# Hybrid decoder layer on one core: the first prompt tile's choice ahead of the sample rows' mixers, its gathers of peer_u beside them, its gathers of peer_v in the second tail

## The chip, the core and the metric

The kernel runs on one core of a Trainium2 chip. The metric is the device time of one execution in microseconds (us). The engines are TensorE (PE; PEld is its loading of weights), VectorE (DVE), ScalarE (ACT), GpSimd (POOL) and SyncE (SP, which issues most DMAs). Gathers of table rows ("indirect DMAs") are issued by POOL.

## What is computed

One decoder layer over 512 prompt rows and 32 sample rows (8 requests of 4), of width 1024. Cut to what matters here:

```
z = x @ w_in -> latent attention (8 heads) and mLSTM memory (4 heads)
  sample rows: latent attention over 2048 cached rows of each request (by page_table),
               and one step of the stored memory state_C
x = layer_norm(ALPHA * x + concat(heads) @ w_out)
x = layer_norm(ALPHA * x + mem_attend(x, ...))          # w_mq, 256 memory tokens, w_mo
q = x @ w_pq; s1, s2 = q @ sub_k1, q @ sub_k2           # 8 heads, 128 keys each
e, g = top 16 of the sums of top 16 of s1 and top 16 of s2; g = softmax
a = g * gelu(x . peer_u[e])                             # 8 x 16 rows of a table of 16384
x = layer_norm(ALPHA * x + sum(a * peer_v[e]))
```

## The kernel before, in words

The prompt is four tiles of 128 rows (0 to 3); the sample rows are tile 4. Group 0 is tile 0 with the sample rows, group 1 is tiles 1, 2 and 3. The last step ("peer") is done in two ways. For tiles 1 and 2 both tables are multiplied whole ("dense"): 128 blocks of peer_u (`u_block`, products `ph`) and 128 blocks of peer_v (`v_block`, products `yd`). For tiles 0, 3 and 4 the chosen rows are gathered: 128 gathers of peer_u and 128 of peer_v for tiles 0 and 3, 32 and 32 for tile 4, each of 128 rows of 1024 floats. A gathered buffer of peer_u (`ru`) is multiplied with the rows and summed by one DVE instruction, a "dot". A gathered buffer of peer_v (`rv`) is summed by eight matmuls `y<-rv,Z`, a "y group", for which DVE writes the weights into `Z`.

The program is one list per engine, in the order in which the code is written, with a paced side list beside it: `te` counts the estimated time of the TensorE instructions that the code writes, and when more than `te.every` has gathered, one step of a second list is written there (`te.start(steps, every)`; `te.finish()` writes the rest at once). `v` does the same by DVE's instructions. Which step stands where on each engine is thus fixed when the program is made.

The stages of before, in order:

- `mixers(0)`: projections, latent attention and mLSTM of group 0. Beside it the keys and values of the memory tokens (`memory`, products `pw`), one step for every 7.0 us.
- `sample_matrix` (the stored state `Ch`, 4 updates of it) and `sample_latent`: 16 iterations, each with four gathers `kvb` of cached rows, 16 transposes of them, copies `kts`, products with `qb` and `qrb`, a maximum (`sst`), the exponential `se`, its transposes, a copy `sPT` and the products `kvb,sPT`.
- `tail("0")` for tile 0: w_out, a layer norm, the memory attention, a layer norm, w_pq (`wz`) and the scores (`sub_k`). The scheduler mixes its first part and the memory's rest into the iterations of `sample_latent`.
- `choices[0].rest()` and `.done()`: the top 16 of tile 0, on DVE, ending with the indices `eT` for the gathers.
- `mixers(1)`, and beside it, after `SKIP` steps, the choice's end and `hidden()`: 128 gathers of `ru` for tile 0 and their dots, one for every 2.6 us.
- `tail("1")` for tiles 1, 2, 3 and the sample rows, with what is left of `hidden()` and, from the end of the tail on, `G`: the other 160 gathers of `ru` and all 288 of `rv`, tile 0's `rv` first.
- The choices of tiles 4, 1, 2 and 3, with the first 40 u blocks; the gates of tiles 1 and 2; and the loop over the 128 v blocks with the other 88 u blocks and the rest of `G`.

Of the kernel before, what the change touches and what calls it, by code (L numbers as in the profile page):

```python
# [18 lines left out]
PSUM = bass.MemoryType.PSUM  # L19
# [174 lines left out]
def program(ctx, tc, I, O, dbg=None):  # L194
# [58 lines left out]
    PN = []  # L253
# [2 lines left out]
    PS = stage.enter_context(tc.tile_pool(name="psum", bufs=4, space=PSUM))  # L256
    stackN, stackC, stackM, stackG, stackX = (ExitStack() for _ in range(5))
    PN.append(stackN.enter_context(tc.tile_pool(name="psum sample", bufs=1, space=PSUM, side="right")))
    SL = stackN.enter_context(tc.tile_pool(name="slat", bufs=1, side="right"))
    DR = ctx.enter_context(tc.tile_pool(name="scratch", bufs=1, space=bass.MemoryType.DRAM))  # L260

    def ps(n=512, name="pm"):
# [5 lines left out]
    def ps3(n=512, name="pc"):  # L268
        return PN[-1].tile([128, n], F32, name=name, tag="pc", bufs=1)
# [42 lines left out]
    right = {}  # L312
# [1164 lines left out]

    def found(i, nh, ef, gt):
        np_ = TOPK * nh
        p = ps3()  # L1480
        te.behind(te.transpose(p[:np_, :128], ef[:, 0], ident))
        te.transpose(p[:np_, 128:256], gt.rearrange("p h k -> p (h k)"), ident)
        if i in DT:
            te.transpose(p[:, 256:384], ef[:, 1], ident)
            v.tensor_copy(iT[i][:, 0:2], p.rearrange("p (a b) -> p a b", b=256)[:, :, :128])
            v.tensor_copy(gT[i], p[:, 128:256])
            s.activation(iT[i][:, 2], p[:, 256:384], AF.Copy, scale=-1.0)
            s.activation(iT[i][:, 3], p[:, 128:256], AF.Copy, scale=-1.0)
        else:
            n = 128 * nh // PH  # L1490
            for a in range(PH // nh):
                v.tensor_copy(eT[i][np_ * a:np_ * a + np_], p[:np_, n * a:n * a + n])
                s.copy(gT[i][np_ * a:np_ * a + np_], p[:np_, 128 + n * a:128 + n * a + n])
# [137 lines left out]
            for w in vs:  # L1631
                self.v_group(*w[1:])

    def hidden(stk):


        X = stk.enter_context(tc.tile_pool(name="hidden", bufs=1, side="right"))
        us = []

        def dot():  # L1640
# [177 lines left out]
    def chooser(T):  # L1818
        def f():
            if T is T0:  # L1820
                stackN.close()
                right["DX"] = ctx.enter_context(tc.tile_pool(name="dense rows", bufs=1, side="right"))
                right["weights"] = ctx.enter_context(tc.tile_pool(name="weights", bufs=1, side="right"))
                right["XG"] = stackX.enter_context(tc.tile_pool(name="rows1", bufs=1, side="right"))
                right["xT1"] = transposed(1, right["XG"])
            else:
                te.finish()
                stackH.close()
                G.open(stackG)
            X = stackC.enter_context(tc.tile_pool(name="choose", bufs=1, side="right"))  # L1830
            for i, c, P in T:
                choices[i] = Choice(i, P, X)
            return X
        return f
# [5 lines left out]
    first_rows(xt0)  # L1840
    for a in range(2):
        nc.scalar.dma_start(lnb0[a], ln_src(0, a))
    MS = stackM.enter_context(tc.tile_pool(name="mixstate", bufs=1))
    Kh = MS.tile([128, H, SEQ], F32, name="Kh")
    vh = MS.tile([128, 4, 512], F32, name="vh")
    mkT = MS.tile([128, MH, SEQ], F32, name="mkT")
# [1 line left out]
    va = MS.tile([128, 4, MH, 129], F32, name="va")  # L1848
    v.memset(va[:, :, :, 128:129], 1.0)

    EVERY0 = 7.0
    with tc.tile_pool(name="group0", bufs=1) as Gp:
        with weights("weights0", 4):
            xT0 = transposed(0, Gp, xt0)
            rows = sample_index(SL)
            te.start(memory(MM, lnb0, xt0), EVERY0)
            with tc.tile_pool(name="q0", bufs=1) as Gq:
                mixT0 = mixers(0, xT0, Gp, Gq)
            with tc.tile_pool(name="smat", bufs=1) as X:
                sample_matrix(X)  # L1860
        sample_latent(SL, *rows)
        te.finish()
        stackF.close()
        with weights("weights0t", 10), tc.tile_pool(name="tail0", bufs=1) as X:
            tail("0", T0, mixT0, Gp, X, chooser(T0))
    DX, XG = right["DX"], right["XG"]
    for i in DT:
        iT[i] = DX.tile([128, 4, 128], F32, name=f"iT{i}")
    LATER = 200
    EVERY = 2.6  # L1870
    EVERY2 = 2.6
    EVERY3 = 1.25
    EVERY4 = 1.75
    EVERY5 = 1.65
    SKIP = 4
    NZ = 2
    W1 = weights("weights1", 2)
    xT1 = right["xT1"]
    with tc.high_priority(-LATER):
        choices[0].rest()  # L1880
    stackC.close()
    G = Gather(stackG, [[(4, 0)], [(3, 32 * q) for q in range(4)]], 3, 6, 3)
    stackH = ExitStack()
    UB0 = 8
    PN.append(stackN.enter_context(tc.tile_pool(name="psum choose", bufs=1, space=PSUM, side="right")))

    def chosen():
        for _ in range(SKIP):
            yield
        choices[0].done()  # L1890
        yield
        yield from hidden(stackH)

    te.start(chosen(), EVERY)
    with tc.tile_pool(name="q1", bufs=1) as Gq:
        mixT1 = mixers(1, xT1, XG, Gq)
    for t, m in zip(mixS, mixT1):
        s.copy(m[:, :, TG:], t)
    W1.close()
    stackM.close()  # L1900
    te.every = EVERY2
    with weights("weights2", 6), tc.tile_pool(name="tail1", bufs=1) as X:
        xT2 = tail("1", T1, mixT1, XG, X, chooser(T1))
    stage.close()
# [14 lines left out]

    v.start(ahead(), EU1)  # L1920
    G.strict = True
    te.start(G.steps(), EVERY3)
    for i in (4,) + DT + (3,):
        choices[i].rest()
        choices[i].done()
# [50 lines left out]
```

## Time and profile before

| | |
|---|---|
| median of 3 runs | 2143.56 us (2138.07 to 2146.85) |
| the profiled execution's own time | 2154.7 us |
| its span (first to last instruction) | 2152.9 us |
| PE busy | 1878.7 us (87%) |
| DVE busy | 1421.5 us (66%) |
| POOL busy | 836.5 us (39%) |
| moved by DMA | 624.85 MB, 290 GB/s over the span |
| mean granted clock of PE | 0.933 |

The span is what the rows below divide; 1.8 us of the execution's own time lie around it. The profiled execution is 0.5% longer than the median. [...]

### The profile page before, as it was taken

The page shows a single profiled execution, that of the slowest core. Times are in us where ns is not written, and L with a number is a line of the kernel's source. Part 1 is how long each engine was busy: PE and PEld are TensorE (multiplying, and loading weights), DVE is VectorE, ACT ScalarE, POOL GpSimd, SP SyncE. Part 2 cuts the span into 40 slices and gives each one's busy share as a digit, 9 for nine tenths or more (in the row PEclk, how much of TensorE's full clock was granted, in tenths as well). Part 3 has the DMA queues.
Part 4 walks back from the last instruction along what each step waited for, and adds up shares of the span by engine and source line. Part 5 has one row for each costly group of instructions (what it writes and reads, how often), then busy time and mean ns, then how long its engine had stood idle before and what let it go on. Part 6 is the DMA issues. An engine that isn't in the chain of part 4 may idle for free. (4 is left out here: it accounts for less than half of the span.)

```text
span 2152.9 us, 32053 instructions
## 1 busy us (share of the span) xinstructions
PE 1878.7 (87%) x11579; PEld 1437.4 (67%) x11579; DVE 1421.5 (66%) x3650; ACT 676.2 (31%) x1349; POOL 836.5 (39%) x715
## 2 busy tenths in 40 slices
PE   6998989878888778688999998879979979999997
PEld 4875656766865666366765675658858767777764
DVE  5234324497778786437899687767666757777666
ACT  2121222232234221212312565434423433444332
POOL 3010233015644424215035444346545646665641
PEclk9988999999978879988999999989989999999999
DMA  9635675728965859756489999999999999999996
GB/s 320 217 88 138 187 242 184 243 82 269 320 227 177 305 161 355 242 207 218 114 280 350 355 383 390 385 338 399 405 329 371 405 342 369 405 405 405 398 370 228
DMA packets 212960, 624.85 MB, mean 290 GB/s; under 512 B 23314, under 2 KB 87890, under 8 KB 198082
## 3 DMA queue, kind: packets, MB, share of 16 engines
q0 software_dynamic: 94272, 327.45, 42.3%
q1 hardware_dynamic: 107120, 279.95, 37.1%
q10 hardware_dynamic: 11410, 15.41, 2.1%
q8 instruction: 92, 1.51, 0.3%
q14 instruction: 66, 0.54, 0.1%
HBM read 592.58 MB, written 30.14 MB: 289 GB/s over the span
## 5 line engine op out<-in xcount | busy, mean ns | idle before, releaser
L241 DVE SCALAR_TENSOR_TENSOR ru<-ru,xr 128x1024 f32<-128x1024 f32 x288 | 349.2, 1220 | 178.7 <-DMA ru<-in_peer_u,idx 138.4
L1516 POOL DMA_INDIRECT rv<-in_peer_v,eT x288 | 340.5, 1182 | 297.4 <-PE y L245 231.9
L1516 POOL DMA_INDIRECT ru<-in_peer_u,idx x160 | 219.8, 1374 | 356.3 <-DVE ru L241 193.2
L1663 POOL DMA_INDIRECT ru<-in_peer_u,idx x128 | 161.5, 1262 | 179.2 <-DVE ru L241 112.2
L245 PE MATMUL ph<-xT2h,utl 128*128 128x256 f32 x704 | 202.8, 288 | 16.9 <-DVE utl L241 16.9
L245 PE MATMUL ph<-xT2l,uth 128*128 128x256 f32 x704 | 202.6, 288 | 0.0
L245 PE MATMUL y<-rv,Z 128*32 128x512 f32 x1152 | 171.8, 633 | 34.4 <-DVE Z L241 19.7
L245 PE MATMUL ph<-xT2h,uth 128*128 128x256 f32 x704 | 200.9, 285 | 0.0
L245 PE MATMUL yd<-vtl,ah 128*128 128x512 f32 x512 | 167.5, 404 | 32.4 <-DVE vtl L241 31.7
L328 ACT CAST vth<-vt 128x1024 fp32r<-128x1024 f32 x128 | 134.4, 1050 | 117.7 <-DMA vt<-in_peer_v 59.1
L245 PE MATMUL yd<-vth,ah 128*128 128x512 f32 x512 | 164.4, 399 | 2.3 <-DVE xa L241 1.4
L241 DVE TENSOR_TENSOR vtl<-vt,vth 128x1024 fp32r<-128x1024 f32 x128 | 156.4, 1222 | 14.5 <-ACT vth L328 12.7
L245 PE MATMUL yd<-vth,al 128*128 128x512 f32 x512 | 164.0, 398 | 0.0
L245 PE MATMUL ph<-xw,ut 128*128 128x256 f32 x640 | 154.5, 387 | 1.2 <-ACT h L1763 1.2
L245 PEld LDWEIGHTS ph<-xT2h,utl 128*128 128x128 f32 x704 | 134.8, 191 | 28.0 <-DVE utl L241 18.7
L328 ACT CAST uth<-ut 128x1024 fp32r<-128x1024 f32 x88 | 92.5, 1051 | 187.3 <-PE ph L245 125.9
L245 PEld LDWEIGHTS ph<-xw,ut 128*128 128x128 f32 x640 | 116.4, 191 | 47.5 <-issue 29.3
L245 PEld LDWEIGHTS yd<-vtl,ah 128*128 128x128 f32 x512 | 95.3, 190 | 77.3 <-DVE vtl L241 40.5
L245 PEld LDWEIGHTS ph<-xT2h,uth 128*128 128x128 f32 x704 | 136.0, 193 | 15.3 <-issue 11.7
L245 PEld LDWEIGHTS ph<-xT2l,uth 128*128 128x128 f32 x704 | 135.6, 193 | 11.7 <-issue 8.4
L245 PEld LDWEIGHTS yd<-vth,al 128*128 128x128 f32 x512 | 96.4, 190 | 35.0 <-issue 15.1
L1086 POOL DMA_INDIRECT kvb<-in_pool_lat,ixk x64 | 63.2, 987 | 135.4 <-PE pn L245 120.2
(542 smaller groups left out, 3712.5 us busy)
## 6 DMA issues: line engine op xcount, KB each, us to landing
vt<-in_peer_v SPq DMA_DIRECT2D x62, 1024.0 KB
ut<-in_peer_ut SPq DMA_DIRECT2D x44, 1024.0 KB
ut<-in_peer_ut SPq DMA_DIRECT2D x40, 512.0 KB
Gd<-stg SPq DMA_DIRECT2D x8, 1984.0 KB
Gt<-Gd SPq DMA_DIRECT2D x31, 512.0 KB
wz<-in_w_z SPq DMA_DIRECT2D x30, 512.0 KB
wo<-in_w_out SPq DMA_DIRECT2D x16, 512.0 KB
wz<-in_w_mq SPq DMA_DIRECT2D x16, 512.0 KB
```

Source lines behind the costliest of these rows:

```text
L241: return lambda out, *a, **k: self.count(f(out, *a, **k), 0.06 + math.prod(out.shape[1:]) / 960)
L245: return self.count(self.e.matmul(out, l, r, **kw), math.prod(r.shape[1:]) * (0.42e-3 if r.dtype == F32R else 1.7e-3))
L328: s.copy(hi, src)
L1086: g.indirect_dma_start(out=t.rearrange("p a b -> p (a b)"), out_offset=None, in_=I["pool_lat"], in_offset=bass.IndirectOffsetOnAxis(ap=ixk ...
L1516: self.last = g.indirect_dma_start(out=t, out_offset=None, in_=I[table], in_offset=bass.IndirectOffsetOnAxis(ap=idx, axis=0))
L1663: g.indirect_dma_start(out=t, out_offset=None, in_=I["peer_u"], in_offset=bass.IndirectOffsetOnAxis(ap=idx[:, k:k + 1], axis=0))
```

## The change

`sample_matrix` and `sample_latent` are written after `tail("0")` and after tile 0's choice. The memory's steps run every 3.2 us and are finished right after `mixers(0)`. `hidden()` starts before `sample_latent`, goes on through `mixers(1)` and is finished at its end. `G` (the gathers for tiles 4 and 3 and tile 0's `rv`) starts ahead of `tail("1")`. Pools are moved to make room; the paces change.

```
-    EVERY0 = 7.0
+    EVERY0 = 3.2
...
                 mixT0 = mixers(0, xT0, Gp, Gq)
-            with tc.tile_pool(name="smat", bufs=1) as X:
-                sample_matrix(X)
-        sample_latent(SL, *rows)
         te.finish()
         stackF.close()
         with weights("weights0t", 10), tc.tile_pool(name="tail0", bufs=1) as X:
             tail("0", T0, mixT0, Gp, X, chooser(T0))
...
-    EVERY = 2.6
-    EVERY2 = 2.6
+    EVERY = 2.4
+    EVERY2 = 2.3
     EVERY3 = 1.25
-    EVERY4 = 1.75
+    EVERY4 = 2.55
     EVERY5 = 1.65
-    SKIP = 4
+    SKIP = 10
...
     with tc.high_priority(-LATER):
         choices[0].rest()
     stackC.close()
...
+    with tc.tile_pool(name="smat", bufs=1) as X:
+        sample_matrix(X)
     te.start(chosen(), EVERY)
+    with tc.tile_pool(name="slat", bufs=1) as X:
+        sample_latent(X, *rows)
...
+    xT1 = transposed(1, XG)
+    W1 = weights("weights1", 2)
     with tc.tile_pool(name="q1", bufs=1) as Gq:
         mixT1 = mixers(1, xT1, XG, Gq)
...
     W1.close()
+    te.finish()
     stackM.close()
-    te.every = EVERY2
+    stackH.close()
+    G.open(stackG)
+    te.start(G.steps(), EVERY2)
     with weights("weights2", 6), tc.tile_pool(name="tail1", bufs=1) as X:
         xT2 = tail("1", T1, mixT1, XG, X, chooser(T1))
...
     G.strict = True
-    te.start(G.steps(), EVERY3)
+    te.every = EVERY3
```

Three places show what moves. On PE, one iteration of `sample_latent` before: the rows with `wo,mixT` are tile 0's w_out, and those with `x` its transposes.

```order
282 L245 MATMUL pn<-kvb,sPT 32x256 x8
283 L248 MATMUL pn<-cst_75,kvb 128x128 x16
284 L245 MATMUL pn<-kts,qb 32x256 x3
285 L245 MATMUL pm<-wo,mixT 128x256
286 L245 MATMUL pn<-kts,qb 32x256 x5
287 L245 MATMUL pn<-krT,qrb 32x128 x8
288 L248 MATMUL pn<-cst_75,se 128x128 x2
289 L248 MATMUL pm<-cst_75,x_3008 128x128 x4
290 L245 MATMUL pn<-kvb,sPT 32x256 x8
```

The same engine in the changed kernel, two iterations:

```order
225 L245 MATMUL pn<-kvb,sPT 32x256 x8
226 L248 MATMUL pn<-cst_81,kvb 128x128 x16
227 L245 MATMUL pn<-kts,qb 32x256 x8
228 L245 MATMUL pn<-krT,qrb 32x128 x8
229 L248 MATMUL pn<-cst_81,se 128x128 x2
230 L245 MATMUL pn<-kvb,sPT 32x256 x8
231 L248 MATMUL pn<-cst_81,kvb 128x128 x16
232 L245 MATMUL pn<-kts,qb 32x256 x8
```

Nothing of the memory, of tile 0's tail or of `mixers(1)` stands between the iterations now; all of `memory` stands inside `mixers(0)`, and tile 0's whole tail before the first iteration.

On DVE, one iteration of the changed kernel (`ru,hh` is a dot of tile 0, the other rows are the iteration's own):

```order
578 L241 SCALAR_TENSOR_TENSOR ru,hh<-ru,xr 128x1024
579 L241 COPY kts<-pn 128x512
580 L241 SCALAR_TENSOR_TENSOR ru,hh<-ru,xr 128x1024
581 L241 COPY kts<-pn 128x512
582 L241 TENSOR_REDUCE sst<-pn 128x1
583 L241 TENSOR_TENSOR sst<-sst 128x1
584 L241 TENSOR_TENSOR sst<-sst,scr 128x1
585 L241 SCALAR_TENSOR_TENSOR ru,hh<-ru,xr 128x1024
586 L241 SCALAR_TENSOR_TENSOR sst<-sst 128x1
587 L241 SCALAR_TENSOR_TENSOR ru,hh<-ru,xr 128x1024
588 L241 SCALAR_TENSOR_TENSOR ob<-ob,sst,pn 128x256
```

Before, no dot stood in `sample_latent`. Now 56 of tile 0's 128 do, three or four to an iteration, and POOL's list has three to five `ru` gathers behind each four `kvb` gathers of 13 iterations. The other 72 stand in `mixers(1)`.

On DVE in the stage of the choices, in the changed kernel (`tv`, `ti`, `rep` and `cd` are steps of a top 16; the dots are tile 4's):

```order
1505 L241 TENSOR_TENSOR cd<-tv_8336 128x8x16
1506 L241 MATCH_REPLACE rep<-tv_8336,sc_8338 128x128
1507 L241 SCALAR_TENSOR_TENSOR ru,hh<-ru,xr 128x1024
1508 L241 MAX tv_8336<-rep 128x8
1509 L241 TENSOR_TENSOR cd<-tv_8336 128x8x16
1510 L241 MAX_INDEX ti_8337<-tv_8336,rep 128x8
1511 L241 SCALAR_TENSOR_TENSOR ru,hh<-ru,xr 128x1024
1512 L241 MATCH_REPLACE rep<-tv_8336,sc_8338 128x128
```

Before, no dot stood among the choices. By the order of the lists, the counts of each stage go as follows (before, then after):

| | `tail("1")` | choices | gates | v loop |
|---|---|---|---|---|
| dots | 73, 0 | 0, 32 | 19, 37 | 141, 91 |
| y groups | 13, 54 | 25, 26 | 24, 8 | 82, 56 |

## Rows read from the trace of the kernel before

**Rows 1.** Windows by stage: start:end, length, busy time of each engine, clock, DMA.

```profile
core 0: us, PE busy (x) PEld busy (x) DVE busy (x) ACT busy (x) POOL busy (x), PEclk, DMA share, GB/s
0.00:166.00 166.00, 142.27 (x849) 117.73 (x853) 65.12 (x254) 32.48 (x101) 27.28 (x35) 0.90 0.61 203
166.00:373.00 207.00, 177.78 (x1587) 126.62 (x1586) 76.01 (x210) 41.97 (x105) 55.24 (x58) 0.95 0.65 192
373.00:441.00 68.00, 60.01 (x411) 53.61 (x403) 38.23 (x154) 16.79 (x49) 0.57 (x1) 0.95 0.61 207
441.00:720.00 279.00, 232.29 (x1201) 190.19 (x1202) 223.53 (x606) 89.08 (x191) 123.06 (x104) 0.87 0.69 223
720.00:1035.00 315.00, 246.34 (x1575) 186.97 (x1574) 194.72 (x415) 70.72 (x126) 98.44 (x85) 0.87 0.72 245
1035.00:1200.00 165.00, 154.79 (x779) 106.08 (x777) 148.46 (x791) 36.51 (x78) 57.45 (x56) 0.99 0.76 269
1200.00:1346.00 146.00, 135.85 (x879) 98.17 (x877) 113.53 (x310) 89.87 (x262) 62.32 (x64) 1.00 0.97 375
1346.00:2153.00 807.00, 729.36 (x4320) 558.03 (x4320) 561.85 (x917) 298.78 (x437) 412.11 (x315) 0.96 0.99 370
```

**Rows 2.** Windows, PE alone: tiles pw (memory); pn (`sample_latent`), two stretches; pm.

```profile
166.00:373.00 207.00, 42.74 (x288) 0.95 0.65 192
...
0.00:166.00 166.00, 17.64 (x131) 0.90 0.61 203
166.00:373.00 207.00, 97.68 (x1060) 0.95 0.65 192
...
166.00:373.00 207.00, 37.48 (x175) 0.95 0.65 192
```

**Rows 3.** Timeline of one latent iteration: start, length, engine, what ended its wait.

```profile
303.81 2.10 PE L248 MATMUL pn<-cst,kvb 128*128 128x128 f32 x16
...
309.94 0.43 DVE L241 TENSOR_REDUCE sst<-pn 128x1 f32<-128x256 f32 x1 [3.87 <-PE pn L245]
...
313.00 1.07 PE L245 MATMUL pn<-kvb,sPT 128*32 128x256 f32 x16
314.00 0.77 PE L248 MATMUL pn<-cst,kvb 128*128 128x128 f32 x5
```

**Rows 4.** The page's costliest groups: dots and two kinds of gathers.

```profile
L241 DVE SCALAR_TENSOR_TENSOR ru<-ru,xr 128x1024 f32<-128x1024 f32 x288 | 349.2, 1220 | 178.7 <-DMA ru<-in_peer_u,idx 138.4
...
L1663 POOL DMA_INDIRECT ru<-in_peer_u,idx x128 | 161.5, 1262 | 179.2 <-DVE ru L241 112.2
...
L1086 POOL DMA_INDIRECT kvb<-in_pool_lat,ixk x64 | 63.2, 987 | 135.4 <-PE pn L245 120.2
```

**Rows 5.** Windows: from the last `sub_k` to tile 0's first gather.

```profile
441.00:490.50 49.50, 40.82 (x210) 34.18 (x211) 44.06 (x185) 17.32 (x33) 6.26 (x11) 0.90 0.29 94
```

**Rows 6.** The tile `Ch`, its updates on DVE: lengths, first and last start.

```profile
L241 DVE TENSOR_TENSOR Ch<-Ch,pm x12: 158/681/689, 202.6 to 221.2; 128x512 f32<-128x512 f32 x8, 128x8 f32<-128x8 f32 x4
```

**Rows 7.** Waits in the v loop (1346 to 2153): us in total, times, longest.

```profile
PE yd L245 <- DVE vtl L241: 31.7, 16, 13.7
PE ph L245 <- DVE utl L241: 16.9, 9, 4.8
...
DVE ru L241 <- DMA ru<-in_peer_u,idx: 124.0, 57, 9.6
```

**Rows 8.** Windows, PE alone: 10 us of `tail("1")` at each of two clocks.

```profile
850.00:860.00 10.00, 6.50 (x24) 0.53 1.02 408
870.00:880.00 10.00, 6.41 (x40) 1.00 0.53 178
```

**Rows 9.** Windows, the best 100 us of the v loop.

```profile
1800.00:1900.00 100.00, 98.70 (x640) 78.62 (x638) 70.20 (x111) 41.77 (x60) 62.01 (x44) 1.00 1.03 407
```

**Rows 10.** Windows of the tile Z: PE (y groups), PEld, DVE (weights written), POOL.

```profile
720.00:1035.00 315.00, 15.53 (x88) 2.82 (x88) 2.19 (x13) 0.34 (x2) 0.87 0.72 245
...
1346.00:2153.00 807.00, 96.40 (x672) 13.69 (x672) 13.34 (x82) 0.00 (x0) 0.96 0.99 370
```

More of the change, by code (lines that the diff above doesn't have):

```diff
@@ L258, in program @@
     PN.append(stackN.enter_context(tc.tile_pool(name="psum sample", bufs=1, space=PSUM, side="right")))
-    SL = stackN.enter_context(tc.tile_pool(name="slat", bufs=1, side="right"))
+    stackH, stackS = ExitStack(), ExitStack()
+    XH = stackH.enter_context(tc.tile_pool(name="hidden", bufs=1))
+    MS = stackM.enter_context(tc.tile_pool(name="mixstate", bufs=1))
+    SL = stackS.enter_context(tc.tile_pool(name="sample", bufs=1))
     DR = ctx.enter_context(tc.tile_pool(name="scratch", bufs=1, space=bass.MemoryType.DRAM))
@@ L1479, in found @@
         np_ = TOPK * nh
-        p = ps3()
+        p = ps3() if i else ps2()
         te.behind(te.transpose(p[:np_, :128], ef[:, 0], ident))
@@ L1632, in steps, with hidden @@
                 self.v_group(*w[1:])
-    def hidden(stk):
-        X = stk.enter_context(tc.tile_pool(name="hidden", bufs=1, side="right"))
+    def hidden(X):
         us = []
@@ L1820, in f @@
             if T is T0:
-                stackN.close()
                 right["DX"] = ctx.enter_context(tc.tile_pool(name="dense rows", bufs=1, side="right"))
[L1823 to L1829, printed above, removed]
             X = stackC.enter_context(tc.tile_pool(name="choose", bufs=1, side="right"))
@@ L1842, in program @@
         nc.scalar.dma_start(lnb0[a], ln_src(0, a))
-    MS = stackM.enter_context(tc.tile_pool(name="mixstate", bufs=1))
     Kh = MS.tile([128, H, SEQ], F32, name="Kh")
@@ L1865, in program @@
             tail("0", T0, mixT0, Gp, X, chooser(T0))
-    DX, XG = right["DX"], right["XG"]
+    DX = right["DX"]
     for i in DT:
@@ L1869, in program @@
     LATER = 200
-    EVERY = 2.6
-    EVERY2 = 2.6
+    EVERY = 2.4
+    EVERY2 = 2.3
     EVERY3 = 1.25
-    EVERY4 = 1.75
+    EVERY4 = 2.55
     EVERY5 = 1.65
-    SKIP = 4
+    SKIP = 10
     NZ = 2
-    W1 = weights("weights1", 2)
-    xT1 = right["xT1"]
+    UB0 = 8
     with tc.high_priority(-LATER):
@@ L1881, in program @@
     stackC.close()
[L1882 to L1885, printed above, removed]
     def chosen():
@@ L1891, in chosen @@
         yield
-        yield from hidden(stackH)
+        yield from hidden(XH)
+    with tc.tile_pool(name="smat", bufs=1) as X:
+        sample_matrix(X)
     te.start(chosen(), EVERY)
+    with tc.tile_pool(name="slat", bufs=1) as X:
+        sample_latent(X, *rows)
+    stackS.close()
+    stackN.close()
+    G = Gather(stackG, [[(4, 0)], [(3, 32 * q) for q in range(4)]], 3, 6, 3)
+    PN.append(stackN.enter_context(tc.tile_pool(name="psum choose", bufs=1, space=PSUM, side="right")))
+    right["weights"] = ctx.enter_context(tc.tile_pool(name="weights", bufs=1, side="right"))
+    XG = right["XG"] = stackX.enter_context(tc.tile_pool(name="rows1", bufs=1, side="right"))
+    xT1 = transposed(1, XG)
+    W1 = weights("weights1", 2)
     with tc.tile_pool(name="q1", bufs=1) as Gq:
```

## The prediction, made before the changed kernel was run

> **What bounds the kernel now.** I read the windows by stage first, then what PE waits for in the longest stage, then one iteration of `sample_latent` in time. The windows [rows 1] show that no single engine bounds the kernel: PE is busy for 142 + 178 + 60 of the first 441 us, and its share stays between 0.78 and 0.95 until the end. What changes is what keeps it from 1. Up to 441 us PE runs short of input only for 61 us in all. In the stage of the choices (1035 to 1200) DVE is busy for 148.5 of 165 us, as full as PE. In the v loop (1346 to 2153) the DMA share is 0.99 and PE idles for 807 - 729 = 78 us. The rows of waits there [rows 7] name DVE's halves of the weights (`vtl` 31.7 us, `utl` 16.9 us), but DVE itself waits 124 us for gathered rows of peer_u: its list is in order, so a dot whose gather is late holds back the halves behind it. The best 100 us of that loop [rows 9] have PE busy for 98.7 at full clock. So the v loop is bound by PE with a surcharge that the gathers impose, and it is what the change lightens.
>
> The iterations of `sample_latent` are a chain of short dependent steps: in one that starts at 303.81, the next starts at 314.00, 10.2 us later [rows 3]. PE's own work for it is 97.68 / 16 = 6.1 us by the tile pn [rows 2]. The rest of PE's 178 us in that stretch is memory (42.74 us) and tile 0's tail with odds and ends (37.48 us) [rows 2]. That other work is the cover of the chain, and the change takes it away.
>
> **The change part by part.**
>
> *To the start of `mixers(1)`, now 441 us.* (a) `mixers(0)`: memory's 42.74 us come in, the prelude of `sample_latent` (17.64 us [rows 2]) goes out, and about 5 us of memory fall into PE's 24 idle us of that stage: 166 + 43 - 18 - 5 = 186. (b) Tile 0's tail: the 68 us of 373 to 441 [rows 1] and what stood in the iterations, at most 37.48 us by pm. Part of that belongs to other pieces, but its layer norm now stands uncovered, so I take the whole: 105 us, which also holds the iterations' last products and the transposes for group 1 that now come behind. (c) Choice, then `sample_matrix`, both on DVE with nearly nothing of PE beside them. Between the last `sub_k` and the first gather 49.5 us passed with DVE busy for 44 [rows 5], `mixers(1)` among it; I take 30 for the choice. The updates of `Ch` ran from 202.6 to about 222, 20 us [rows 6]. Sum 50, bounds 40 and 64. (d) The prelude: 17.64 us of PE and its waits, 22. (e) Sixteen iterations alone. Without cover the chain is a little shorter than 10.2 us, since about a microsecond of w_out stood between the last product and the maximum: 9.5. Onto DVE come 56 dots, 3.5 for each iteration, at 1.22 us [rows 4] and about 0.08 for reading the sum: 4.6 us. DVE has long gaps in an iteration, but a dot in front of `kts`, of the maximum or of `sPT` delays the chain by what is left of it. I take 1.5 us for all of them: 11.0 for each, 176. The bounds are 9.5 (all dots hidden) and 14.1 (none hidden). POOL is below that: four kvb at 0.99 and 3.5 ru at 1.26 us [rows 4] make 8.4. Sum: 186 + 105 + 50 + 22 + 176 = 539, which is **+98**; the bounds of (c) and (e) alone make +64 to +162.
>
> *`mixers(1)`* loses the choice (30 us of DVE) and 11 dots (83 in the trace's window, 72 by the lists). PE is busy for 232 of 279 us and DVE for 224 [rows 1], so DVE's relief buys only waits: **-12**, bounds -30 and 0.
>
> *`tail("1")`* gets 43 more y groups (54 by the lists, against 88 matmuls, 11 groups, in the trace) and loses its dots. A group costs 15.53 / 11 = 1.41 us here, 96.40 / 84 = 1.15 in the v loop [rows 10]: 49 to 61 us of PE. PE idles for 69 of this stage's 315 us [rows 1], mostly for weights; a group written ahead of a matmul whose weights are late lies in that wait. I let a little over half of them hide: **+25**, bounds 0 and +60, the upper one if the gathers make the weights later by as much as the groups hide.
>
> *Choices and gates.* 32 dots come into a stage where DVE is busy for 148.5 of 165 us: 32 x 1.30 = 42, and layer norms of the finished tiles, less the 16 us that DVE has free: +35. The gates lose 16 y groups at about 1.2 us and gain 18 dots, with DVE busy for 113 of 146 us and DMA at 0.97 with about as many gathers as before (69 against 64): 0. Together **+35**, bounds +20 and +50.
>
> *The v loop* loses 26 y groups x 1.15 = 30 us of PE, and 50 dots x 1.30 = 65 us of DVE. Of the 102 gathers fewer, each 128 x 1024 x 4 bytes, come 53.5 MB; at the window's 370 GB/s they are 145 us of DMA, so DMA stops being full, and the gathers that remain land earlier. I take two thirds of PE's 78 idle us as won (52), and 3 us from the clock, 0.96 here [rows 1]: **-85**. Bounds: -50 (the groups and a quarter of the idle time) and -137 (groups, all idle time, and 0.04 x 729 = 29 us of clock).
>
> Sum: 98 - 12 + 25 + 35 - 85 = +61. The profiled execution took 2154.7 us, so the changed one takes 2216; the median of before stands at 2143.56 / 2154.7 = 0.995 of its profiled execution, which gives **2205 us** as a median. Put shortly: 128 dots and 102 gathers are moved to where DMA and DVE are free, but the chain that they are moved beside is laid bare, and its cost appears whole.
>
> **The rivals.**
>
> *The v loop gives back all that it can, and the iterations hide the dots: faster.* The best 100 us [rows 9] speak for it: with gathers in time, PE is never idle and at full clock. The v loop is then at -137 and the iterations at 9.5 us (-24 on my sum), `tail("1")` hides all but 10 us of its groups. 61 - 52 - 24 - 15 = -30: **2113 us**. It decides from the point at which the v loop gains 146 us with all else as I have it, or 130 with the iterations at 10 us. Against it: 91 dots stay in the loop, each still ahead of a half that PE needs.
>
> [...]
>
> *The cover is replaced: no change.* If the choice, 30 us, and `sample_matrix`, 20, run in part beside tile 0's own last products and the prelude (their lists are in order on each engine, but the engines are not bound to each other), (c) and (d) shrink by 30, and with the v loop at -115 the sum is +1: **2145 us**.
>
> **How the numbers follow.** I give my forecast (2150 to 2245) a chance of 0.62, the low clock 0.10, no change 0.10, and faster 0.18. A measurement of this kernel can tell about 0.5% (11 us) from no change. The forecast and the low clock are both slower: 0.72. The likeliest time is 2205. The range takes in the bounds of the iterations upward without the whole of the low clock, and most of the faster rival downward: 2122 to 2262.
>
> **What would show it.** In the profile after, `wt1`, the first weights of `mixers(1)`, should start at about 539 us (505 to 600). From the first `kvb` transpose to the last `kvb,sPT` there should be about 176 us, with PE busy for near 55% and dots between `kts` and the maximum. A stretch of about 50 us ahead of it has DVE full and PE nearly idle. The stage of the choices should be at about 200 us with DVE above 0.9. The v loop should take about 720 us with DMA under 0.95 and DVE's wait for `ru` well under 124 us. The prediction is wrong if the iterations keep to 10 us or less and the v loop falls to 680, or if their clock is near 0.5.

## The result, and the profile after

The changed kernel takes 2312.73 us (median of 4 runs, 2297.72 to 2324.36) against 2144.56 us before (median of 4 runs): 1.079 times as long, 95% interval 1.072 to 1.086. Slower was forecast, but by 61 us and not by 168, and the time lies outside the range. The profiled execution has a span of 2314.7 us, 161.8 more than before, which the stages share out so (boundaries by the first or last matmul of a tile, us):

| stage | before | after | difference | forecast |
|---|---|---|---|---|
| to the first `wt1` of `mixers(1)` | 441.3 | 600.0 | +158.7 | +98 |
| `mixers(1)` | 279.0 | 265.0 | -14.0 | -12 |
| `tail("1")` | 331.5 | 364.4 | +32.9 | +25 |
| choices | 147.8 | 212.9 | +65.1 | +35 with the gates |
| gates | 152.9 | 180.8 | +27.9 | |
| v loop to its last product | 789.4 | 680.6 | -108.8 | -85 |

The choices and the gates are best read together: 136 products `ph` of the u blocks, some 33 us of PE, stand in the choices now and stood in the gates before.

The windows of the changed kernel by stage answer to [rows 1]; the first six are the stretch up to `mixers(1)`: `mixers(0)`, tile 0's tail, choice with `sample_matrix`, prelude, iterations, and what follows them.

```profile
core 0: us, PE busy (x) PEld busy (x) DVE busy (x) ACT busy (x) POOL busy (x), PEclk, DMA share, GB/s
0.00:187.00 187.00, 163.23 (x1004) 140.84 (x1004) 60.03 (x211) 30.06 (x91) 9.31 (x17) 0.93 0.60 192
187.00:275.00 88.00, 75.12 (x472) 67.85 (x472) 37.98 (x148) 12.01 (x37) 3.51 (x5) 0.96 0.76 257
275.00:333.00 58.00, 27.89 (x116) 15.80 (x115) 41.87 (x202) 2.40 (x7) 2.70 (x3) 0.60 0.47 113
333.00:370.70 37.70, 19.88 (x134) 15.03 (x133) 12.25 (x56) 7.27 (x18) 14.24 (x16) 0.50 0.50 166
370.70:571.00 200.30, 124.13 (x1062) 74.38 (x1058) 113.53 (x243) 39.92 (x93) 131.65 (x118) 0.76 0.70 234
571.00:600.00 29.00, 10.55 (x69) 7.81 (x61) 17.76 (x43) 5.80 (x17) 16.06 (x15) 0.50 0.97 320
600.00:865.00 265.00, 229.30 (x1202) 190.12 (x1201) 179.52 (x421) 86.25 (x187) 87.40 (x65) 0.86 0.50 173
865.00:1229.00 364.00, 310.35 (x1997) 211.56 (x1996) 171.45 (x445) 68.77 (x128) 141.02 (x132) 0.90 0.81 275
1229.00:1442.00 213.00, 173.00 (x822) 121.67 (x820) 173.76 (x783) 34.58 (x75) 83.65 (x83) 0.91 0.85 301
1442.00:1623.00 181.00, 115.25 (x620) 91.82 (x618) 137.57 (x350) 93.24 (x265) 69.79 (x63) 0.77 0.78 273
1623.00:2314.00 691.00, 673.15 (x4111) 547.27 (x4110) 497.06 (x758) 300.20 (x432) 246.09 (x203) 0.99 0.93 344
```

Read it from the bottom: the v loop is now PE's alone, busy for 673 of 691 us, and DMA is down to 0.93. That is what the change buys. It pays at the top: between 275 and 600 us PE works for 182 of 325 us, at a granted clock of 0.50 to 0.76, where the kernel before had 0.95 [rows 1]. The waits of the iterations, PE's first and then DVE's, name what PE waits for:

```profile
PE pn L248 <- ACT se L1114: 29.2, 16, 3.0
PE pn L248 <- DVE ob L241: 21.2, 8, 4.7
PE pn L245 <- DVE sPT L241: 12.8, 8, 4.7
...
DVE ru L241 <- DMA ru<-in_peer_u,idx: 44.3, 22, 4.6
```

The first is the chain (maximum, exponential). The next two are copies and sums on DVE that come late because of what stands ahead of them in its list, and the last row says what: dots whose gathers have not landed. The timeline of one iteration shows it happen:

```profile
454.82 0.44 PE L248 MATMUL pn<-cst,se 128*128 128x128 f32 x2 [1.69 <-ACT se L1114]
455.93 0.94 POOL L1665 DMA_INDIRECT ru<-in_peer_u,idx  x1 [0.30 <-issue]
457.21 1.23 DVE L241 SCALAR_TENSOR_TENSOR ru<-ru,xr 128x1024 f32<-128x1024 f32 x1 [3.22 <-DMA ru<-in_peer_u,idx]
...
458.49 0.42 DVE L241 COPY sPT<-pn 128x256 f32<-128x256 f32 x1
...
458.97 1.94 PE L245 MATMUL pn<-kvb,sPT 128*32 128x256 f32 x16 [3.71 <-DVE sPT L241]
...
461.15 0.94 POOL L1089 DMA_INDIRECT kvb<-in_pool_lat,ixk  x1 [4.28 <-PE pn L245]
```

The transposes of `se` are done by 455.3, but the copy `sPT` stands behind a dot that waits 3.2 us for its gather, and so `kvb,sPT` starts at 458.97. POOL's next `kvb` gather waits for that product to free a buffer, and the `ru` gathers of the next dots stand behind it. DVE's part stands in the two rows: the copy starts at 458.49, as the dot ends (457.21 + 1.23), 3.2 us after the transposes. The sixteen iterations came at distances of 8.4 to 19.1 us, from one `kvb,sPT` to the next. The matmuls are slow too: `kvb,sPT` takes 1.94 us for 16 where it took 1.07 [rows 3], at the mean granted clocks of 0.76 and 0.95 of the two stretches.

### The profile page after: what moved, and what is told of

Its sections match the earlier page's. It is cut to its first block, busy times and chain, and to the rows that moved or that the text cites. A ratio compares the mean times of both kernels' runs of the same rounds, so it can differ in the third digit from the quotient of the medians.

```text
span 2314.7 us, 32073 instructions
## 1 busy us (share of the span) xinstructions
PE 1921.9 (83%) x11579; PEld 1484.2 (64%) x11579; DVE 1442.8 (62%) x3650; ACT 680.5 (29%) x1346; POOL 805.4 (35%) x715
## 5 line engine op out<-in xcount | busy, mean ns | idle before, releaser
L1519 POOL DMA_INDIRECT rv<-in_peer_v,eT x288 | 333.5, 1158 | 484.0 <-PE y L245 422.6
L1519 POOL DMA_INDIRECT ru<-in_peer_u,idx x160 | 185.5, 1159 | 329.8 <-DVE ru L241 219.6
L1665 POOL DMA_INDIRECT ru<-in_peer_u,idx x128 | 157.5, 1230 | 80.2 <-DVE ru L241 40.5
L245 PE MATMUL yd<-vtl,ah 128*128 128x512 f32 x512 | 162.1, 394 | 2.9 <-DVE vtl L241 2.9
L241 DVE TENSOR_TENSOR utl<-ut,uth 128x1024 fp32r<-128x1024 f32 x88 | 107.7, 1224 | 72.8 <-ACT uth L331 72.8
L245 PEld LDWEIGHTS ph<-xw,ut 128*128 128x128 f32 x640 | 123.4, 199 | 40.1 <-issue 20.5
L245 PE MATMUL pgt<-O,O 128*128 128x128 f32 x512 | 94.9, 338 | 56.2 <-DVE O L241 48.3
L245 PEld LDWEIGHTS ph<-xT2h,utl 128*128 128x128 f32 x704 | 132.2, 188 | 10.2 <-issue 8.4
L245 PEld LDWEIGHTS pgt<-O,O 128*128 128x128 f32 x512 | 81.5, 233 | 72.5 <-DVE O L241 42.5
```

The source lines that it names most:

```text
L241: return lambda out, *a, **k: self.count(f(out, *a, **k), 0.06 + math.prod(out.shape[1:]) / 960)
L245: return self.count(self.e.matmul(out, l, r, **kw), math.prod(r.shape[1:]) * (0.42e-3 if r.dtype == F32R else 1.7e-3))
L1519: self.last = g.indirect_dma_start(out=t, out_offset=None, in_=I[table], in_offset=bass.IndirectOffsetOnAxis(ap=idx, axis=0))
L1665: g.indirect_dma_start(out=t, out_offset=None, in_=I["peer_u"], in_offset=bass.IndirectOffsetOnAxis(ap=idx[:, k:k + 1], axis=0))
```

## Experiments

The kernel before was run again beside each group of runs, with medians of 2139.7 to 2158.5 us; ratios are to those runs. "Iterations" is the time from the first `kvb` transpose to the last `kvb,sPT`; the changed kernel has 200 us, and runs with the same list there took up to 218.

**The two parts of the change apart.** `e4_gathers_only` leaves the kernel before as it is, and draws only the gathers forward:

```
+        stackH.close()
+        G.open(stackG)
+        opened.append(1)
+        yield from G.steps()          # behind hidden(), in tail("1")
...
-    EVERY = 2.6
-    EVERY2 = 2.6
+    EVERY = 1.9
+    EVERY2 = 1.8
...
-    EVERY4 = 1.75
+    EVERY4 = 2.3
```

> The kernel before, with its latent iterations left beside tile 0's tail, and only the gathers drawn forward: hidden() every 1.9 us in mixers(1), and as soon as it has ended, in the middle of tail(1), the other gathers behind it, every 1.8 us there, the v loop at 2.3. It has 45 y groups in the second tail where the changed kernel has 54, and 95 dots in the v loop where that has 91. If the loss of the change is the uncovered chain, this version keeps the gain: mixers(1) starts at 441 us, the v loop takes 690 to 730 us, and the whole 2080 to 2120 us. Rival (the second tail, the choices and the gates take back what the v loop gives): 2130 to 2190 us.

2192.49 us, 1.020 of before (1.014 to 1.025): the rival's, 2 us above its range. Its windows from `mixers(1)` on, stage by stage:

```profile
439.80:728.40 288.60, 232.57 (x1205) 189.10 (x1203) 229.13 (x616) 88.52 (x191) 133.97 (x109) 0.86 0.68 222
728.40:1113.30 384.90, 307.18 (x1934) 208.94 (x1932) 214.99 (x519) 72.75 (x132) 155.39 (x150) 0.87 0.83 293
1113.30:1317.50 204.20, 174.71 (x828) 120.00 (x827) 173.34 (x784) 34.61 (x75) 94.03 (x91) 0.93 0.91 328
1317.50:1493.90 176.40, 118.78 (x659) 93.08 (x658) 137.65 (x352) 92.31 (x264) 69.60 (x62) 0.81 0.81 291
1493.90:2184.00 690.10, 678.89 (x4126) 548.16 (x4126) 493.84 (x756) 298.53 (x431) 249.75 (x210) 1.00 0.94 349
```

The v loop wins its 99 us, as expected, but `mixers(1)` gives back 10, the second tail 53, the choices 56 and the gates 24. So the gathers and what moves with them cost 143 us where they go and gave 99 where they came from. This alone is +43 us.

`e12_latent_only` is the other part: the order of the changed kernel, with no gather beside the iterations and those that follow at the paces of before.

```
             m = v.transpose(idx, eT[0][:, sl])
+            if q == 0:
+                v.after(m, te.last)        # not ahead of mixers(1)
...
+        while not late:
+            yield
...
-    te.finish()
-    G.open(stackG)
-    te.start(G.steps(), EVERY2)
+    te.every = EVERY2                      # G from chooser(T1) on, as before
```

> Only the first part of the change: the memory, sample_matrix and sample_latent stand where the changed kernel has them, but no gather stands beside the iterations; hidden() runs in mixers(1) and tail(1) and all other gathers from the end of that tail, at the paces of before. Theory: the change's loss is the sum of two, the bared chain and the gathers drawn forward (the run with those alone lost 43 us). Then mixers(1) starts at 545 to 560 us, all later stages take what they take in the kernel before within 15 us, and the whole is 2240 to 2270 us. Rival (the gathers drawn forward do harm only together with the moved iterations): 2290 us or more here or under 2220.

Its two executions took 2228.8 and 2263.9 us, 35 us apart. The same kernel again:

> The latent part of the change alone, once more, since its two executions lay 35 us apart. If the two parts of the change add up (43 us for the gathers drawn forward alone, 165 for both), it is 1.04 to 1.06 of before, with all stages from tail(1) on within 10 us of before.

2232.62 us, 1.039 of before (1.034 to 1.045), +93 us. From `tail("1")` on each stage is within 3 us of before (331.8, 145.3, 152.0 and 786.8 us), so the loss lies wholly ahead: the second tail starts at 804.9 us in place of 720.3. 93 and 43 make 136 of the 168 us; the other 32 come only when both stand together. That is not much more than the three intervals leave open (12 to 15 us each), and e4 draws the gathers forward at other paces and puts none of them beside the iterations. The profiled executions say where the rest arises: to the start of the second tail the changed kernel loses 144.7 us, e16 84.6 and e4 8.1, so 52 are left over there, while the stages behind it lose 11 less than the two parts apart. Only in the changed kernel do dots stand among the bared iterations; e6 below prices them at 37 us.

**Is it the clock?** `e1_cover` adds work on PE to each iteration of the changed kernel:

```
+                cover(2)      # behind the kts copies
+                cover(4)      # behind the products with krT
+                cover(2)      # behind the transposes of se
...
+                nc.tensor.matmul(pd[:, :256], ident, wuk[:, 0], start=True, stop=True)
```

> The changed kernel, with eight products added to each latent iteration on PE whose results nobody reads (128x256, as many as w_out and the transposes gave an iteration of the kernel before): two ahead of the products with kts, four behind those with krT, two behind the transposes of se. Theory CLOCK (the iterations took 12.5 us and not 11 because PE alone fell to the low clock, 0.76 in that stretch): the clock of the stretch rises to 0.93 or more, an iteration takes 10.5 to 11.5 us although PE has more to do, and the whole is 15 to 30 us shorter than the changed kernel. Rival DOTS (the dots and gathers stand in the chain): the iteration stays at 12 us or more whatever the clock, and the whole is the same or longer.

The window of its iterations:

```profile
369.70:599.50 229.80, 175.04 (x1294) 109.25 (x1294) 118.30 (x251) 41.37 (x94) 130.83 (x124) 0.85 0.65 217
```

The clock rises from 0.76 to 0.85 only, the iterations take 230 us and not 200, and the whole 2326.26 us (1.082). The added products lengthen the chain by more than a better clock gives back. So a better clock, bought with more work on PE, mends nothing. The 0.93 that the theory asked for was not reached, and how much of the 200 us the clock makes was not separated.

**Is it the dots?** Three runs change what stands beside the iterations. `e2_no_dots_beside` only writes `hidden()` later, without the tie that e12 has:

> The changed kernel, with tile 0's gathers of peer_u and their dots held back until mixers(1) starts (where they come every 1.6 us in place of 2.4). Rival DOTS: the iterations fall from 12.5 to 10.5 us or less, 30 us for the sixteen, at a clock still under 0.8. Theory CLOCK: they stay at 11.5 us or more, since PE is no busier. mixers(1) gets 56 more dots, so it should be 20 to 70 us longer, and the whole says nothing by itself: the stretch of the iterations does.

2331.54 us (1.084), iterations 210 us. It does not answer the question, because the scheduler drew most of the gathers ahead again: 48 dots still stand in that stretch, where the changed kernel has 58. `e6_none_beside` adds the tie:

> The changed kernel, with the gathers of peer_u for tile 0 tied behind the first products of mixers(1), so that none of them and no dot stands beside the iterations (in the run with hidden() written later, 48 of 58 dots still came there). In mixers(1) they come every 1.6 us. Theories WAIT and RUN: the sixteen iterations take 145 to 165 us (9 to 10.3 each). Theory CLOCK: 185 us or more, at a clock of 0.8 or less. mixers(1) and tail(1) get the 56 dots back and take 20 to 60 us more.

Its windows: the iterations, `mixers(1)` and the second tail; then two of PE's waits in the iterations.

```profile
373.90:537.00 163.10, 113.46 (x1062) 71.43 (x1058) 48.80 (x123) 37.24 (x90) 52.92 (x56) 0.82 0.32 94
554.20:835.70 281.50, 234.44 (x1202) 190.64 (x1200) 222.61 (x514) 89.51 (x192) 157.25 (x125) 0.86 0.78 259
835.70:1236.50 400.80, 313.00 (x1997) 212.30 (x1998) 200.52 (x493) 71.26 (x131) 162.80 (x148) 0.86 0.81 280
...
PE pn L248 <- ACT se L1114: 40.0, 16, 3.4
...
PE pn L245 <- DVE sPT L241: 4.1, 8, 0.5
```

Now the iterations come every 9.9 to 10.9 us (the last after 7.9), 163 us in all, at a clock of 0.82: the dots and gathers beside them cost 37 us or more, 2.3 us for each iteration or 0.65 us for each dot. PE's wait for `ob` is gone and that for DVE's `sPT` fell from 12.8 to 4.1 us, so those two were the dots' doing; the wait for `se`, the chain's own, is left. But `mixers(1)` takes 281.5 us (265.0) and the second tail 400.8 (364.4), so that the whole is 2329.71 us (1.083), no better. At this pace (1.6 us in place of 2.4) the dots cost about as much in the two stages behind, 53 us, as beside the iterations.

`e5_dots_behind` ties each dot to the PE instruction written last when the dot was written, and `e7_kvb12` has `bufs=12` for `kvb`:

> The changed kernel, with each dot of tile 0 ordered behind the PE instruction that had been written last when the dot was written, so that it stands eight gathers behind its own gather and cannot be drawn ahead. Theory WAIT (in the changed kernel every second iteration takes 14 to 19 us and the others 10.5, because a dot that waits for its gather stands in DVE's list ahead of sPT or kts; the gather is late since it stands in POOL's list behind kvb gathers, which wait for buffers that the chain itself frees): DVE's wait for ru in the stretch of the iterations falls from 44 us to under 15, and the sixteen take 165 to 180 us in place of 200. Rival RUN (the dots' own 1.3 us in the chain are the cost): the wait falls but the sixteen stay above 190 us. Some dots move from mixers(1) into tail(1).

> The changed kernel, with twelve kvb buffers in place of eight, so that POOL waits later for the iterations to free them and reaches the ru gathers behind them sooner. Theory WAIT: DVE's wait for ru in that stretch falls under 30 us and the sixteen take 170 to 190 us. If they stay within 5 us of 200, the kvb buffers are not what makes the gathers late.

Both fell short. In e5 the dots wait for PE in place of DMA (30.8 us in 23 waits), the iterations take 235 us and the whole 2337.26 (1.087). In e7 DVE's wait for `ru` falls from 44 to 25 us, but the iterations take 217 and the whole 2319.59 (1.079, interval 1.067 to 1.090). Three runs with the changed kernel's own list there (e3, e9 and e11) had 30 to 32 us of that wait and took 216 to 218 us, longer than the 200 with 44; so the wait for `ru` alone does not set the length. That dots with late gathers hold the chain up is shown by e6; that earlier gathers would cure it is not.

**Is it the chain?** Two iterations in flight change the order of the iterations' own steps; `e13_latent_two` does it to e12, `e14_after_two` to the changed kernel, `e15_before_two` to the kernel before. Two things go with it: `kvb` has twelve buffers in place of eight (not in e15), and two of the iteration's products are written to another set of PSUM buffers.

```
+        for it, nx in zip(its, its[1:]):
+            next(nx)          # gathers, transposes, kts of the next
+            next(it)          # transposes of se, sPT of this one
+            next(nx)          # products, maximum, exponential of the next
+            next(it, None)    # kvb,sPT of this one
```

> The run with the latent part of the change alone, with two iterations in flight: the transposes of the next stand ahead of the transposes of se, its products ahead of kvb,sPT, and there are twelve kvb buffers. Theory CHAIN (the bared iterations take 10.0 to 10.2 us because each waits for its own maximum, exponential and copies, while PE has 6 us to do): an iteration takes 6.5 to 8 us, the sixteen 105 to 130 us in place of 160, and the whole falls by 30 to 55 us. Rival CLOCK or POOL (PE's low clock, or the gathers of kvb, hold the pace): the sixteen stay above 145 us.

The window of e13's iterations:

```profile
372.50:470.90 98.40, 89.25 (x1063) 59.29 (x1060) 47.68 (x125) 35.35 (x90) 49.14 (x52) 0.97 0.50 146
```

98 us where e16 has 143, 6.2 us for an iteration: PE is busy for 89 of them, and its clock is at 0.97. 2189.34 us, 1.021 of before (1.017 to 1.026). The same iterations and gathers at the same place: the order of the steps and the buffers it needs were worth 44 us, and the clock rose with them (0.90 in e16). In e16 PE waits 25.2 us for `se`, in e13 1.4. Twelve buffers alone were not tried on e16, but PE waits for no `kvb` gather there, and on the changed kernel they won nothing (e7). PE's busy time fell from 109 to 89 us, of which some 9 are first products of `mixers(1)` that stood among e16's iterations; the rest are the same matmuls in less time, so a part of the 44 may be the clock's (0.97 in place of 0.90), which was not separated.

> The changed kernel with the same two iterations in flight and twelve kvb buffers. POOL issues four kvb and about 3.5 ru gathers for an iteration at some 1.25 us each, 9.4 us. If POOL's list and the dots' waits now hold the pace, an iteration takes 9.5 to 11.5 us, the sixteen 150 to 185 us in place of 200 to 218, and the whole 2265 to 2300 us. If the chain alone held it, the sixteen fall to 130 us or less.

The iterations fall to 116 us, below what POOL's list was thought to allow, since fewer dots now stand among them (20 in place of 58), and `mixers(1)` takes 308 us with the others (265). 2285.01 us, 1.069 (1.065 to 1.073), 28 us better than the changed kernel.

> The kernel before with two iterations in flight (eight kvb buffers, since twelve do not find room). Its iterations are covered by the memory and tile 0's tail, and PE is busy there for 177 of 206 us. If the cover is whole, nothing is to be had: within 10 us of before. If the chain still costs in the iterations that no other work is left for, mixers(1) starts 10 to 25 us earlier and the whole is 2125 to 2140 us.

2215.91 us, 1.036 (1.032 to 1.039): worse. With the eight `kvb` buffers that fit there, the next iteration's gathers are issued only as the last one's products free them, and PE waits for them 46.6 us between 160 and 460 us, where the kernel before has no such wait:

```profile
PE pn L248 <- DMA kvb<-in_pool_lat,ixk: 46.6, 30, 6.6
```

**The prelude, and what is bared ahead of it.** In the changed kernel's timeline POOL issues the first gather of rope keys at 329.69 us, and PE's waits between 325 and 372 us show the price (us, times, longest):

```profile
329.69 1.54 POOL L1029 DMA_INDIRECT krb<-in_pool_rope,ixr  x1 [56.75 <-DVE iT L241]
```

```profile
PE pn L248 <- DMA krb<-in_pool_rope,ixr: 13.3, 4, 9.9
```

`e9_rope_early` issues them in `mixers(0)`, into eight buffers of their own.

> The changed kernel, with the eight gathers of cached rope keys (krb) issued in mixers(0) into buffers of their own, in place of two buffers that are only free when sample_matrix is over (there the first was issued at 329.7 us and PE waited 13.3 us for them). If the late pool is what stretched the prelude, it falls from 38 to 22 to 27 us and the whole by 8 to 15 us; if the prelude is bound by its own short steps at the low clock, it stays above 33 us.

The prelude falls from 38 to 24.8 us, as expected, but the iterations behind it take 216 us, and the whole 2312.22 us (1.072, 1.061 to 1.084): nothing is won that can be told. `e18_two_and_early` is e13 with this and with `sample_matrix` back behind `mixers(0)`.

> The latent part alone with two iterations in flight, and with the two pieces that the moved stage had laid bare ahead of it put back: sample_matrix right behind mixers(0), where memory's last steps cover it, and the rope gathers in mixers(0) into buffers of their own, so that the choice of tile 0 is the only thing left on DVE between tile 0's tail and the iterations. Theory (what the move lost was the bare steps, not the order as such): mixers(1) starts at 420 to 450 us in place of 478, and the whole is 20 to 60 us under the run with two iterations alone (2189 us): 2125 to 2170 us, at or below the kernel before. Rival (the pieces cost the same wherever they stand): 2175 to 2200 us.

2187.27 us, 1.021 (1.017 to 1.025): the rival's. The prelude starts as soon as tile 0's tail is over, but that tail ends 52 us later, as `sample_matrix` was put in front of it; `mixers(1)` starts at 474.8 us in place of 478.5.

**The choices and the gates.** `e3_slow_choices` is the changed kernel with `EVERY3` and `EVERY5` at 3.5 and `EVERY4` at 1.9; `e11_no_dots_choices` calls `G.known` only after the last choice:

```
         choices[i].done()
-        G.known.add(i)
+    G.known.update((4,) + DT + (3,))
```

> The changed kernel, with the gathers in the stages of the choices and the gates slowed (one step for every 3.5 us of PE in place of 1.25 and 1.65) and those of the v loop quickened (1.9 in place of 2.55): 18 dots fewer among the choices, 16 fewer in the gates, 34 more in the v loop. If the choices and gates are longer than before by the dots that came into them, they go from 213 and 181 us to 165 to 190 and 150 to 165, the v loop grows by 20 to 60 us, and the whole is 10 to 50 us shorter. Rival (the two stages wait for transfers and for a slow PE clock, not for dots): they keep within 10 us of 213 and 181, and the whole grows by what the v loop grows.

> The changed kernel, with the gathers for tiles 4 and 3 held back until the last choice is done, so that the choices have 10 y groups and no dot beside them (26 and 32 in the changed kernel). If the dots and their waits for gathers are what made that stage 65 us longer than before, it falls from 213 to 140 to 160 us, the gates stay within 15 us of 181, and the v loop grows by 30 to 50 us from 681. Rival (what is left of the dense work, the u blocks and their loads, sets that stage): it stays above 190 us.

The windows of e3:

```profile
1228.10:1391.10 163.00, 145.87 (x658) 113.28 (x657) 148.52 (x725) 34.07 (x74) 40.23 (x39) 0.94 0.71 246
1391.10:1525.90 134.80, 106.39 (x643) 86.51 (x642) 112.94 (x305) 91.27 (x263) 31.86 (x30) 0.89 0.70 256
```

The first row is the choices, the second the gates (213 and 181 us in the changed kernel); the choices of e11 are this row:

```profile
1229.60:1363.10 133.50, 121.74 (x555) 92.44 (x555) 125.64 (x685) 31.68 (x68) 17.14 (x18) 0.97 0.55 193
```

e3 takes 2277.42 us, 1.059 (1.055 to 1.063), 35 better than the changed kernel although its iterations took 218 us: 50 and 46 us are won in the two stages, and the v loop pays 60. In e11 the choices fall by 79 us. Some 30 of these are u blocks that moved on into the gates (454 products `ph` in the choices in place of 584), and the gates, with 40 dots (37 in the changed kernel), took them in without growing: 181.6 us. But 44 gathers were left for the end, behind the last v block, where they took some 90 us with nothing but their own sums beside them: 2331.61 (1.081). `e17_after_mended` joins e11 to two iterations in flight, with `EVERY4` at 1.95 so that they fit.

> The changed kernel with two iterations in flight, and with the gathers for tiles 4 and 3 held back until the last choice is done (v loop at 1.95 in place of 2.55, so that all of them fit). If the two savings add up (28 us of the one, and of the other the 64 us that the stages of choices, gates and v loop gave, less some 30 us of gathers that had been left for the end), it takes 2220 to 2260 us. If gathers cost about the same in every stage, it stays at 2270 to 2300.

2259.09 us, 1.054 (1.049 to 1.059), the best of the changed order with the gathers drawn forward. The choices take 135 us, the v loop 736: 26 us better than e14.

**The paces of the kernel before.** Two runs move gathers without moving anything else, `e8_before_slow` (3.5, 1.45 and 3.5 for `EVERY3`, `EVERY4` and `EVERY5`) and `e10_before_fast` (1.0, 1.95 and 1.4):

> The kernel before, with the gathers of the choices and the gates slowed (3.5 us for a step in place of 1.25 and 1.65) and those of the v loop quickened (1.45 in place of 1.75). In the run of the changed kernel with such paces a gather taken out of the choices gave 1.1 us and out of the gates 1.4, and one put into the v loop cost 0.8. By those prices some 50 gathers taken from each of the two stages give 55 and 70 us, and a hundred more in the v loop cost 80: 2080 to 2120 us. Rival (the v loop of before is already full of transfers at a share of 1.00, so that there a gather costs its 1.3 to 1.5 us of transfer): 2140 to 2190 us.

> The kernel before, with quicker gathers among the choices (1.0 in place of 1.25) and in the gates (1.4 in place of 1.65) and slower ones in the v loop (1.95 in place of 1.75): 9 more y groups among the choices, 12 more dots in the gates, 12 dots and 2 groups fewer in the v loop. In the run with slow gathers a gather cost 0.3 us among the choices, 0.6 in the gates and 1.2 in the v loop. By those prices this is 10 to 20 us shorter than before: 2125 to 2140 us. Rival (dots in the choices and gates stand in front of DVE's own work and cost twice that): 2150 to 2180 us.

e8 takes 2222.68 us (1.034, 1.029 to 1.038), the rival's: 46 gathers fewer among the choices give 14 us, 33 fewer in the gates 20, and 75 more in the v loop, where the DMA share is 1.00, cost 91. e10 takes 2159.37 us (0.9995, 0.995 to 1.004): the v loop gains 32 us, the choices lose 16 and the gates 14. No version that was run beats the kernel before.

## Why the forecast had the sign and missed the size

Right: that the v loop ceases to be held by its gathers (-109 where -85 was said; PE's wait for `vtl` and `utl` fell from 49 us [rows 7] to under 4), that the chain of `sample_latent` was covered and would appear whole, and `mixers(0)` (186 us said, 187.0 measured), `mixers(1)` (-12, -14) and the second tail (+25, +33). In the v loop PE's idle time fell as said (54 us, 52 said), and nearly all of the 24 us beyond the forecast is its busy time, which fell by 54 where 33 was said. That `mixers(1)` came out so near is partly luck: 22 dots left it (83 and 61 in the traces) where 11 were counted. What failed is the price of what was moved: three terms of the sum counted how long moved instructions run, and left out most of what they wait for. By its own bounds the stretch up to `mixers(1)` just held (+64 to +162 said from (c) and (e) alone, +158.7 measured); the choices and gates did not (+20 to +50 said, +93 measured).

*Term (e), the iterations: 176 us said, 200 measured (218 in other runs of the same list).* "9.5 us without cover" is 10.2 in e6, and 8.9 in e16, where a part of `mixers(1)`'s first products stood among them. "1.5 us for all dots" is 2.3, and 3.4 in the runs with 218 us. The dots were priced by what is left of a dot that runs; the trace shows 44 us of dots that stand in the list and wait. That a dot waits for its gather had been read in the v loop [rows 7] and was not carried over to the place to which dots were moved.

*Terms (b) to (d), what surrounds the iterations: 177 us said, 213 measured.* Term (b), 105 us, was 117: 88 for the tail and 29 behind the iterations. Term (c), 50, was 58, within its bounds; term (d), 22, was 38. The prelude waits 13.3 us for rope keys and the end 9.8 us for the rows `x0d`. Before, these loads were issued from 15.5 and from 379.9 us on, 115 us ahead of the first use of the one and 61 us ahead of `mixers(1)`; now they were issued from 329.7 and 580.9 us on, as the stage they belong to began. The prediction moved instructions and forgot that a moved stage leaves its prefetch behind; with the rope keys issued early (e9) the prelude takes 24.8 us.

*Choices and gates: +35 said, +93 measured.* 32 dots were priced at 42 us, and DVE's busy time in the choices did grow by 40. But the 16 us that DVE had free were subtracted, and in the result they are not used: its idle time grows by 25, of which 22 are the dots' waits for their gathers. Of the choices' +65 the u blocks that came from the gates are about half, if their PE time counts in full, and what is left for the dots is near the 35 that was said. The larger miss is the gates, put at 0. By PE's work they should have become some 54 us shorter (32 of `ph`, 22 of y groups) and they are 28 longer.

The rows: the wait of DVE in the choices; the products `ph` in the choices, before and after, and in the gates, before and after; PE's wait for DVE's `O` in the gates, before and after.

```profile
DVE ru L241 <- DMA ru<-in_peer_u,idx: 22.2, 19, 5.1
...
L245 PE MATMUL ph<-xw,ut 128*128 128x256 f32 x448 | 105.5, 387 | 1.2 <-ACT h L1763 1.2
L245 PE MATMUL ph<-xw,ut 128*128 128x256 f32 x584 | 138.9, 395 | 3.8 <-DMA ut<-in_peer_ut 3.8
L245 PE MATMUL ph<-xw,ut 128*128 128x256 f32 x192 | 49.0, 385 | 0.0
L245 PE MATMUL ph<-xw,ut 128*128 128x256 f32 x57 | 16.7, 410 | 0.0
...
PE pgt L245 <- DVE O L241: 1.4, 4, 0.5
PE pgt L245 <- DVE O L241: 48.3, 31, 8.1
```

In the gates PE waits 48.3 us for DVE's `O`, in a list with 37 dots where 19 stood. e3 bears it out: with 16 dots fewer there that wait is 11.9 us and the stage 134.8 us. So does e11: with 40 dots and 130 more products `ph` in them the gates stay at 181.6 us, so it is not PE's work that sets their length.

Of the rivals, the low clock, which the two clocks of [rows 8] suggest, came true in part. The granted clock of the iterations was 0.76 where the covered ones had 0.95 [rows 1], `kvb` transposes took 421 ns in the median and not 273, and between 275 and 600 us the clock was 0.50 to 0.76. e13 shows the converse: with the chain filled from itself it is at 0.97, and the transposes take 273 ns. No run shows the sixteen iterations at half the clock; the lowest is 0.70 (e5). As a cause by itself e1 does not bear it out, nor does e1 exclude it. The faster rival had its v loop, nearly (-109 of -137), and nothing else. "No change" wanted terms (c) and (d) to shrink by 30 us; they came to 96, 24 more than said.

What stays open: why the iterations of kernels with the same list there took 200 to 218 us (at clocks of 0.76 and 0.71 to 0.73), how much of the iterations' time is the clock's, and whether all of the 32 us by which the two parts together lose more than apart are the dots among the bared iterations.

## What to carry to other kernels

Before moving a chain of small dependent steps out of its cover, count what PE does in it: here 6.1 us [rows 2] of the 10.2 that a bared iteration took (e6). Then ask what else could stand between its steps, its own next iteration first of all (6.2 us for an iteration in e13). Work that is "moved to where the engine is free" must be priced with its waits: here DVE waited 44.3 us for gathers among the iterations, with its next instructions behind the waiting dots, and the 58 dots cost the stretch 37 us or more. And look at when the moved stage's loads can now be issued: the rope keys, whose buffers stand in that stage's own pool, were issued from 329.7 us on in place of 15.5, and PE waited 13.3 us for them.

## What the runs showed of the hardware

A gather of 128 rows with its dot or half of a y group (a group sums two gathered buffers: 144 groups for the 288 gathers of peer_v) had a price that differed by stage: 1.2 us in the v loop of before, where the DMA share is 1.00 (e8, 76 more for 91 us), 0.9 us in the same loop with it at 0.94 to 0.98 (e3, 70 more for 60 us), 1.4 us in the choices and gates of the changed kernel (e3, 70 fewer for 96 us) and 0.4 us in those of before (e8, 79 fewer for 35 us). The two stages are taken together because u blocks move between them. The mix differs too, 34 dots and 17 groups in e3 and 19 dots and 29 groups in e8, and was not separated from the stage. The same loop of 16 iterations ran at granted clocks of 0.82 bare (e6), 0.76 with dots (the changed kernel) and 0.97 with two in flight (e13), with PE busy for 113, 124 and 89 us for the same matmuls and idle for 50, 76 and 9: where they were least interrupted by waits, their records were shortest.
